# Neighbourhood attention on 64x64 quarters of the array, SSD norm scales spread by DMA, and another start, in a one-layer hybrid encoder

## The chip, the cores and the metric

The program runs on one core of one Trainium2 chip. The metric is the device time of one execution in microseconds; lower is better. All arithmetic results are float32; the large projections are written as three products of a rounded high part and a low remainder (fp32r operands), the small ones as plain float32 matmuls.

## The reference

One encoder layer for two sequences of 256 tokens, 1024 channels, handled together as 512 tokens. What matters here:

```python
x = x + 0.5 * swiglu(rms_norm(x, ffn1_norm), ffn1_w_gate, ffn1_w_up, ffn1_w_down)
u = rms_norm(x, mix_norm)
proj = u @ w_in
q_na, k_na, v_na, q_mem, z, xbc, dt_raw, gate_logits = split_sizes(proj, IN_SIZES)
...
o_na = neighborhood_attention(q_na, k_na, v_na, na_rpb)     # 16 heads of 64; grid of 4 rows x 64 columns
...
y_ssd = y_fwd + y_bwd + ssd_d[:, None] * xs                 # 32 heads of 64
y_ssd = y_ssd.reshape(bsz, t, D_INNER) * silu(z)
o_ssd = grouped_rms_norm(y_ssd, ssd_norm, SSD_GROUPS)       # 8 groups of 256 channels
...
merged = g_na*(o_na @ w_br_na) + g_ssd*(o_ssd @ w_br_ssd) + g_mem*(o_mem @ w_br_mem)
x = x + merged @ w_out
x = x + 0.5 * swiglu(rms_norm(x, ffn2_norm), ffn2_w_gate, ffn2_w_up, ffn2_w_down)

def neighborhood_attention(q, k, v, rpb):                   # for each row r, column block n of 16 queries
    s = einsum("bnqhd,brnkhd->bhnqrk", q_r, k_b) * scale     # keys: 4 rows x 32 columns = 128
    s = where(valid, s + bias, -1e30)                        # 16 columns of the 32 are valid for a query
    p = softmax(s over the 128 keys)
    o = einsum("bhnqrk,brnkhd->bnqhd", p, v_b)
```

## The kernel before

**Weights and the main matmuls.** Weights come from HBM in items of up to 512 KB (`fetch`, line 288) into a ring of nine buffers, eight items ahead. `ahead` rounds an item to a high part on ScalarE (line 320, tile `wh`) and leaves the remainder on VectorE (line 234, tile `wl`), at most three items ahead. TensorE then runs three 512-wide matmuls for each 128x128 block: high weights with the high part of the activations, high with low, low with high (lines 543 to 545, 565, 587 to 589, 607 to 609). The order of the work is the list `PLAN`. Work that is not in the list (norms, attention, SSD) is written as generators; after each entry of the list each of up to three (later four) active ones is advanced by one `yield`. A tile framework puts the instructions into each engine's queue in an order of its own, close to the written one, and each engine takes its queue in that order; so does SyncE, which issues all DMAs.

**The start** (`setup`, `warm`). SyncE loads the first eight channel tiles `x` and the first weights. `warm` (line 427) runs ten matmuls on a zeroed tile `af` meanwhile. `factor_x` multiplies a half of an `x` tile by the norm gain, rounded on ScalarE (line 249, tiles `sh`, `a2h`) and its remainder on VectorE (line 245, `sl`, `a2l`); `t_x` makes further combinations, and `t_squares` sums the squares of all `x` tiles (tile `sq`). The first two passes over the weights (`do_pl`, lines 607 to 609, tile `q`) take four chunks of 24 matmuls each. A small product, `sum` (line 504), which TensorE takes within the first chunk of the second pass, turns the sum of the squares into one value a token.

**Neighbourhood attention** (`t_na`, one generator for each of eight head pairs). The queries of two heads are transposed (line 952) and copied into two zeroed tiles `qbd`, block diagonal in the two heads, so that for each of four column blocks one 128x128 by 128x128 matmul gives the scores of both heads (line 984, tile `ns`). The bias tile is added on VectorE (line 245), a maximum is taken (989), ScalarE takes the exponentials, VectorE divides, TensorE transposes (1001, tile `nT`), ScalarE copies, and one 128x128 by 128x128 matmul a column block gives the outputs of both heads (1007, tile `no`), of which the diagonal quarters are kept. The two sequences (`b`) go one after the other, with three yields between. These small tiles and the transposed ones share a pool of three PSUM banks (`pd`).

**SSD norm** (end of `t_ssd`, eight groups). The squares are summed by `sum` (line 504), a reciprocal root is taken in small VectorE steps (`rsqrt`, lines 270 to 276), giving a value a token, spread over partitions. `spread` (line 512) makes four diagonal tiles `dg`, and `spread_mm` (line 521, tile `R`) multiplies them by a tile of ones, so that every partition holds the row of all 512 values. Two multiplications by `R` (line 245) follow. The groups below `KEEP` = 6 are then stored to HBM (`scr_o`).

Of the kernel before, what the change touches and what calls it, by code (L numbers as in the profile page):

```python
# [24 lines left out]
NEG = -1e30  # L25
KEY0 = (0, 8, 24, 32)
STRIP0 = (16, 8, 8, 0)
# [151 lines left out]
KEEP, EARLY, PG, LEND = 6, 4, 54, 4  # L179
# [3 lines left out]
class Layer:  # L183
# [126 lines left out]
    def ahead(self, ci):  # L310

        for i in range(self.n_split, min(ci + 3, len(ITEMS))):
            it = ITEMS[i]
            self.fetch(i + DEPTH)
# [5 lines left out]
            self.S.copy(hi[:, :n], t[:, :n])  # L320
# [54 lines left out]
    def setup(self):  # L375
# [18 lines left out]
        self.namask = c(8).rearrange("p (n k) -> p n k", n=4)  # L394
# [5 lines left out]
        self.scr_x = self.dr.tile([KD, 128, NT], F32, name="scr_x")  # L400
        self.scr_v = self.dr.tile([NT, D], F32, name="scr_v")
        self.scr_r = self.dr.tile([2, 32, 2, 256], F32, name="scr_r")
        self.scr_o = self.dr.tile([16, 128, NT], F32, name="scr_o")
        self.xs_start("ffn1")
        for k in range(KD):
            if k < 4:
                self.factor_x(1, k, k, 0)
                self.factor_x(0, k, k, 1)
            else:
                self.factor_x(2, k - 4, k, 0)  # L410
                self.factor_x(4, k - 4, k, 1)
            if k % 2 and k < 5:
                self.ahead(k // 2 - 2)
# [7 lines left out]
    def warm(self):  # L421

        z = self.g(p="af")
        self.G.memset(z, 0.0)
        ps = self.bank("wm")
        for _ in range(WARM):
            self.T.matmul(ps[:, :256], z[:, :128], z[:, :256], start=True, stop=True)
# [507 lines left out]
    def t_na(self, pr):  # L935
        V, S, T = self.V, self.S, self.T
        hf, lp = divmod(pr, 4)
        vt = [self.g(p="nv").rearrange("p (n c) -> p n c", n=4) for _ in range(2)]
        sv = self.scr_v
        for b in range(2):  # L940
            for n in range(4):
                src = bass.AP(sv.tensor, sv.offset + (b * 256 + KEY0[n]) * D + pr * 128, [[64 * D, 4], [D, 32], [1, 128]])
                self.nc.sync.dma_start(out=vt[b][:, n, :], in_=src)
        st = self.g(p="st")
        self.nc.sync.dma_start(out=st[:, :192], in_=self.a["strip"][pr])
        qbd = [self.g(p="qbd") for _ in range(2)]
        for z in qbd:
            self.G.memset(z, 0.0)
# [4 lines left out]
        pv = ps.rearrange("p (b r n c) -> p b n r c", b=2, r=4, n=4)  # L953
        for b in range(2):
            qv = qbd[b].rearrange("p (n h r c) -> p n h r c", n=4, h=2, r=4)
            for h in range(2):
                rows = slice(64 * h, 64 * h + 64)
                self.ts(qv[rows, :, h, :, :], pv[rows, b], self.par("qn", 0, rows), ALU.mult)
# [6 lines left out]
        bias = self.g(p="bi")  # L965
        bv = bias.rearrange("p (n r k) -> p n r k", n=4, r=4)
        sv4 = st[:, :192].rearrange("p (r k) -> p r k", r=4)
        for n in range(4):
            self.tt(bv[:, n], sv4[:, :, STRIP0[n]:STRIP0[n] + 32],
                    self.namask[:, n:n + 1, :].to_broadcast([128, 4, 32]), ALU.add)  # L970
        yield
        if pr < LEND:
            self.lent += 1
            on = self.pf.tile([128, 1024], F32R, tag="raw", name=self.name("on"))
            hi, lo = on[:, :512], on[:, 512:]
        else:
            hi, lo = self.g(F32R, "onh"), self.g(F32R, "onl")
        self.o[("on", pr)] = (hi, lo)
        for b in range(2):
            ps = self.bank("ns")  # L980
            q4 = qbd[b].rearrange("p (n q) -> p n q", n=4)
            kv = kT[:, b * 256:(b + 1) * 256].rearrange("p (r k) -> p r k", r=4)
            for n in range(4):
                T.matmul(ps[:, n * 128:(n + 1) * 128].rearrange("p (r k) -> p r k", r=4), q4[:, n, :],
                         kv[:, :, KEY0[n]:KEY0[n] + 32], start=True, stop=True)
            t_ = self.g(p="nt")
            self.stt(t_, ps, 0.125, bias, ALU.mult, ALU.add)
            mx, sm, rc = (self.small(4, "nm") for _ in range(3))
            V.tensor_reduce(out=mx, in_=t_.rearrange("p (n k) -> p n k", n=4), op=ALU.max, axis=AX.X, negate=True)
            for n in range(4):  # L990
                v = t_[:, n * 128:(n + 1) * 128]
                self.act(v, v, AF.Exp, bias=mx[:, n:n + 1], accum_out=sm[:, n:n + 1])
            yield
            V.reciprocal(rc, sm)
            for n in range(4):
                v = t_[:, n * 128:(n + 1) * 128]
                self.ts(v, v, rc[:, n:n + 1], ALU.mult)
            yield
            ps = self.bank("nT")
            for n in range(4):  # L1000
                T.transpose(ps[:, n * 128:(n + 1) * 128], t_[:, n * 128:(n + 1) * 128], self.ident)
            pT = self.g(p="npT")
            S.copy(pT, ps)
            yield
            ps = self.bank("no")
            for n in range(4):
                T.matmul(ps[:, n * 128:(n + 1) * 128], vt[b][:, n, :], pT[:, n * 128:(n + 1) * 128], start=True, stop=True)
            for h in range(2):
                rows = slice(64 * h, 64 * h + 64)
                ov = ps[rows].rearrange("p (n h q) -> p n h q", n=4, h=2)[:, :, h, :].rearrange("p n (r c) -> p n r c", r=4)  # L1010
                dst = lambda z: z[rows, b * 256:(b + 1) * 256].rearrange("p (r n c) -> p n r c", r=4, n=4)
                S.copy(dst(hi), ov)
                self.tt(dst(lo), ov, dst(hi).bitcast(F32), ALU.subtract)
            if b == 0:
                yield


    def do_gate(self, key, cis):
# [180 lines left out]
    def t_ssd(self, g):  # L1199
        V, S, T = self.V, self.S, self.T  # L1200
# [85 lines left out]
                y.append(q)  # L1286
            yield
        self.tt(y[0], y[0], y[1], ALU.add)
        ps = self.rows_to_cols(y[0])
        dg = self.spread(self.rsqrt(ps[:, 0:4], 4, 1.0 / 1024))  # L1290
        yield
# [28 lines left out]
def layout(inp):  # L1320
# [41 lines left out]
    qcol = n[None, :] * 16 + (i % 16)[:, None]  # L1362
    kcol = np.array(KEY0)[:, None] + kc[None]
    start = np.clip(qcol - 8, 0, 48)
    ok = (kcol[None] >= start[:, :, None]) & (kcol[None] < start[:, :, None] + 16)
    c[:, 1024:1152] = np.where(ok, 0.0, NEG).reshape(128, 128)

    rpb = f("na_rpb")[0]
    h = i // 64
    r = i // 16 % 4  # L1370
    rel = np.clip(np.arange(48)[None] - (i % 16)[:, None] - 1, 0, 30)
    row = np.arange(4)[None] - r[:, None] + 7
    strip = np.stack([rpb[(2 * pr + h)[:, None, None], row[:, :, None], rel[:, None, :]] for pr in range(8)])
    return {"w": w, "xT": chan("x_prompt", "x_sample"), "memT": chan("mem_prompt", "mem_sample"), "params": p,
            "consts": c, "strip": np.ascontiguousarray(strip.reshape(8, 128, 192))}


def build(arrays):
# [18 lines left out]
```

## Time and profile before

| | |
|---|---|
| median of 3 runs (lowest to highest) | 1771.69 us (1771.17 to 1771.84) |
| the profiled execution's own time | 1770.46 us |
| its span, from the first to the last instruction | 1768.7 us |
| TensorE matmuls busy | 1752.2 us, 99% of the span |
| VectorE, ScalarE, GpSimd busy | 71%, 48%, 1% |
| TensorE clock granted, mean | 0.998 |
| bytes moved by DMA | 206.77 MB, 117 GB/s on the mean |

Busy time of TensorE is a union of intervals whose ends are modelled, so it does not say that the array works at its peak. What a stage costs is read from the distance between the starts of its matmuls, and a float32 matmul (not fp32r) stands in the trace as two records, a transpose or an fp32r matmul as one. "L984" is line 984 of the kernel before. In a timeline a row gives start, length, engine, line and tiles (written tile, an arrow, read tiles), the count of merged records, and in brackets the idle time of the engine before it with what ended that.

### The profile page before, as it was taken

To read this page: it belongs to the slowest core of one execution; us is meant where nothing else is said; L and a number is where in the kernel's file an instruction comes from. 1 tells how busy PE (TensorE), PEld (TensorE's weight loads), DVE (VectorE), ACT (ScalarE), POOL (GpSimd) and SP (SyncE) were. 2 spreads that over 40 slices of the span, in tenths; PEclk is the share of its full clock that TensorE was granted. 3 is DMA by queue.
4 is the path that set the end of the run, shared out by engine and by line. 5 is a ranking of instruction groups with operands and counts; after the bars stand their busy time and mean duration, and the time that the engine had idled before them with its cause. 6 is when DMAs were issued, how large, how long until landed. Compare 5 with 4: busy or idle time off the path is not lost.

```text
span 1768.7 us, 22285 instructions
## 1 busy us (share of the span) xinstructions
PE 1752.2 (99%) x8348; PEld 1437.9 (81%) x8348; DVE 1252.4 (71%) x2128; ACT 855.3 (48%) x1530; POOL 9.0 (1%) x21
## 2 busy tenths in 40 slices
PE   8999999999999999999999999999999999999999
PEld 6888888988788888888787777777788878888887
DVE  7676776876554376857878988888743697776775
ACT  6444443543223335445656666667632464444442
POOL 0000000000000000000000000000000000000000
PEclk9999999999999999999999999999999999999999
DMA  6143334442323231323333433345434234244331
GB/s 254 48 150 131 101 110 141 155 155 80 96 84 100 80 115 58 105 88 98 119 119 124 138 131 120 113 143 173 143 127 136 84 98 140 84 144 130 98 117 48
DMA packets 75675, 206.77 MB, mean 117 GB/s; under 512 B 7856, under 2 KB 17456, under 8 KB 75568
## 3 DMA queue, kind: packets, MB, share of 16 engines
q1 hardware_dynamic: 75568, 205.36, 35.5%
q8 instruction: 65, 1.06, 0.2%
q14 instruction: 42, 0.34, 0.1%
HBM read 195.76 MB, written 9.57 MB: 116 GB/s over the span
## 4 chain that ended last, share of the span: by engine, by line
PE 96%; DVE 3%; DMA 1%; ACT 0%; issue 0%; SPq 0%; DVEq 0%; ACTq 0%
PE ac L565 20%; PE m L543 12%; PE m L545 12%; PE m L544 11%; PE q L587 5%; PE q L589 5%; PE q L588 5%; PE d L544 5%; PE d L545 5%; PE d L543 5%; PE y L1272 2%; PE hT L690 1%; DMA wr<-in_w 1%; DVE wl L234 1%; PE CB L1222 1%; PE q L608 1%
## 5 line engine op out<-in xcount | busy, mean ns | idle before, releaser
L320 ACT CAST wh<-wr 128x1024 fp32r<-128x1024 f32 (+1 forms) x357 | 371.3, 1040 | 689.2 <-PE ac L565 167.4
L234 DVE TENSOR_TENSOR wl<-wr,wh 128x1024 fp32r<-128x1024 f32 (+1 forms) x357 | 431.3, 1208 | 254.3 <-ACT wh L320 244.2
L543 PE MATMUL m<-uh,wh 128*128 128x512 f32 (+1 forms) x584 | 234.3, 401 | 1.4 <-ACT tg L249 1.4
L565 PE MATMUL ac<-wh,sh 128*128 128x512 f32 (+1 forms) x616 | 229.3, 373 | 0.8 <-ACT wh L320 0.8
L565 PE MATMUL ac<-wl,sh 128*128 128x512 f32 (+1 forms) x616 | 228.1, 370 | 0.7 <-DVE wl L234 0.7
L545 PE MATMUL m<-uh,wl 128*128 128x512 f32 (+1 forms) x584 | 228.4, 391 | 0.0
L544 PE MATMUL m<-ul,wh 128*128 128x512 f32 (+1 forms) x584 | 228.3, 391 | 0.0
L565 PE MATMUL ac<-wh,sl 128*128 128x512 f32 (+1 forms) x616 | 228.1, 370 | 0.0
L544 PE MATMUL d<-hl,wh 128*128 128x512 f32 x352 | 137.2, 390 | 0.7 <-DVE hl L234 0.7
L543 PE MATMUL d<-hh,wh 128*128 128x512 f32 x352 | 137.4, 390 | 0.5 <-ACT hh L256 0.5
L545 PE MATMUL d<-hh,wl 128*128 128x512 f32 x352 | 137.0, 389 | 0.0
L543 PEld LDWEIGHTS m<-uh,wh 128*128 128x128 f32 (+1 forms) x584 | 109.2, 187 | 30.7 <-issue 3.5
L565 PEld LDWEIGHTS ac<-wl,sh 128*128 128x128 f32 x616 | 116.1, 189 | 20.7 <-DVE wl L234 1.2
L565 PEld LDWEIGHTS ac<-wh,sh 128*128 128x128 f32 x616 | 116.0, 188 | 20.8 <-ACT wh L320 1.7
L565 PEld LDWEIGHTS ac<-wh,sl 128*128 128x128 f32 x616 | 116.1, 188 | 19.6
L545 PEld LDWEIGHTS m<-uh,wl 128*128 128x128 f32 (+1 forms) x584 | 109.2, 187 | 25.7 <-issue 1.5
L544 PEld LDWEIGHTS m<-ul,wh 128*128 128x128 f32 (+1 forms) x584 | 109.4, 187 | 21.9
L245 DVE SCALAR_TENSOR_TENSOR x<-d,x 128x512 f32<-128x512 f32 x96 | 66.2, 690 | 76.5 <-PE d L545 76.1
L234 DVE TENSOR_TENSOR wr<-wr,wr 128x1024 f32<-128x1024 f32 x80 | 97.6, 1220 | 6.6 <-DMA wr<-in_w 5.6
L587 PE MATMUL q<-wh,uh 128*128 128x512 f32 x256 | 101.9, 398 | 0.0
L589 PE MATMUL q<-wl,uh 128*128 128x512 f32 x256 | 99.9, 390 | 0.0
L588 PE MATMUL q<-wh,ul 128*128 128x512 f32 x256 | 99.8, 390 | 0.0
(252 smaller groups left out, 2932.1 us busy)
## 6 DMA issues: line engine op xcount, KB each, us to landing
wr<-in_w SPq DMA_DIRECT2D x308, 512.0 KB
rw<-scr_r SPq DMA_DIRECT2D x64, 256.0 KB
nv<-scr_v SPq DMA_DIRECT2D x64, 64.0 KB
scr_o<-cv SPq DMA_DIRECT2D x12, 256.0 KB
or<-scr_o SPq DMA_DIRECT2D x12, 256.0 KB
wr<-in_w SPq DMA_DIRECT2D x9, 256.0 KB
x<-in_xT SPq DMA_DIRECT2D x8, 256.0 KB
mr<-in_memT SPq DMA_DIRECT2D x8, 256.0 KB
```

The costliest lines, as they stand in the source:

```text
L234: self.V.tensor_tensor(out=out, in0=a, in1=b, op=op)
L245: self.V.scalar_tensor_tensor(out=out, in0=a, scalar=s, in1=b, op0=op0, op1=op1)
L320: self.S.copy(hi[:, :n], t[:, :n])
L543: self.T.matmul(ps[:m], wh[:, kk, :], xh, start=i == 0, stop=False)
L544: self.T.matmul(ps[:m], wh[:, kk, :], xl, start=False, stop=False)
L545: self.T.matmul(ps[:m], wl[:, kk, :], xh, start=False, stop=i == n - 1)
L565: go = lambda l, r, **f: self.T.matmul(ps, l, r, skip_group_check=True, **f)
L587: self.T.matmul(self.qb[t], xh, wh[:, kk, :], start=k == 0, stop=False)
L588: self.T.matmul(self.qb[t], xl, wh[:, kk, :], start=False, stop=False)
L589: self.T.matmul(self.qb[t], xh, wl[:, kk, :], start=False, stop=k == KD - 1)
L608: self.T.matmul(qb[t], xl, wh[:, kk, :], start=False, stop=False)
L1272: T.matmul(yb[64 * hp:64 * hp + 64, b * 256:(b + 1) * 256], xt[i][:, (2 * b + st) * 128 + 64 * hp:(2 * b + st) * 128 + 64 * hp + 64], w[hp ...
```

## The change

Four parts.

1. *Attention scores and outputs by quarters.* The queries of both heads stay on one tile (head h on partitions 64h to 64h+63). For each sequence, column block and head a matmul with 64 rows (one head's channels), 64 columns (64 queries) and 128 moving columns (keys) gives the scores; head h goes to its own PSUM bank, column blocks alternate between the lower and the upper 64 output partitions. The outputs take 64-column weights (one head's values of a block) and 64 moving columns, head h to output partitions 64h and up. Both sequences of a head pair go through in the same step, with three yields in all where there were seven. `qbd` is no longer zeroed. The bias comes laid out in full from the host.
2. *SSD norm, groups 0 to 5.* The 128x4 tile of scales is stored to HBM by one DMA (512 values of 4 bytes, token by token) and read back by a second one, spread over 128 partitions; the multiplication then reads that tile, two yields later. Groups 6 and 7 stay as they were.
3. *The start.* `factor_x` of a pair of `x` tiles stands right behind the loads of that pair, and `ahead` behind it; the weights beyond are fetched later (`self.depth`). A one-column ScalarE copy of the zeroed tile stands ahead of the idle matmuls and makes ScalarE load its function table then.
4. `WARM` goes from 10 to 16.

```diff
-RING, DEPTH, WARM = 9, 8, 10
+RING, DEPTH, WARM = 9, 8, 16
...
-        self.x = [self.g(p="x") for _ in range(KD)]
+        self.x, self.depth = [], 0
+        self.xs_start("ffn1")
         self.warm()
...
         for c in range(4):
             for k in (2 * c, 2 * c + 1):
+                self.x.append(self.g(p="x"))
                 dma(out=self.x[k], in_=self.a["xT"][:, k, :])
             self.fetch(c)
+            for k in (2 * c, 2 * c + 1):
+                for p, r in ((1, 0), (0, 1)) if c < 2 else ((2, 0), (4, 1)):
+                    self.factor_x(p, k % 4, k, r)
+            if c < 3:
+                self.ahead(c - 2)
+        self.depth = DEPTH
...
         z = self.g(p="af")
         self.G.memset(z, 0.0)
+        self.act(z[:, :1], z[:, 1:2], AF.Copy)
...
+        ps = [self.bank("ns") for _ in range(2)]
         for b in range(2):
-            ps = self.bank("ns")
...
             for n in range(4):
-                T.matmul(ps[:, n * 128:(n + 1) * 128].rearrange("p (r k) -> p r k", r=4), q4[:, n, :],
-                         kv[:, :, KEY0[n]:KEY0[n] + 32], start=True, stop=True)
+                g, c0 = n % 2, b * 256 + n // 2 * 128
+                for h in range(2):
+                    rows = slice(64 * h, 64 * h + 64)
+                    T.matmul(ps[h][64 * g:64 * g + 64, c0:c0 + 128].rearrange("p (r k) -> p r k", r=4),
+                             qT[rows, b * 256 + n * 64:b * 256 + n * 64 + 64], kv[rows, :, KEY0[n]:KEY0[n] + 32],
+                             start=True, stop=True)
...
-            for n in range(4):
-                T.matmul(ps[:, n * 128:(n + 1) * 128], vt[b][:, n, :], pT[:, n * 128:(n + 1) * 128], start=True, stop=True)
+        for b in range(2):
             for n in range(4):
+                c0 = b * 256 + n * 64
+                for h in range(2):
+                    T.matmul(ps[64 * h:64 * h + 64, c0:c0 + 64], vt[b][:, n, 64 * h:64 * h + 64], pT[h][:, c0:c0 + 64],
+                             start=True, stop=True)
...
-        dg = self.spread(self.rsqrt(ps[:, 0:4], 4, 1.0 / 1024))
-        yield
-        ps = self.spread_mm(dg)
+        r = self.rsqrt(self.rows_to_cols(y[0])[:, 0:4], 4, 1.0 / 1024)
+        if g < KEEP:
+            yield
+            self.link(99)
+            self.nc.sync.dma_start(out=self.scr_n[g].rearrange("t p -> p t"), in_=r)
+            ps = self.g(p="rw")
+            sn = self.scr_n
+            self.nc.sync.dma_start(out=ps, in_=bass.AP(sn.tensor, sn.offset + g * 512, [[0, 128], [1, 512]]))
+            yield
+            yield
+        else:
+            dg = self.spread(r)
+            yield
+            ps = self.spread_mm(dg)
```

What that makes of the engines' queues, at three places. First ScalarE at the very start, before (numbers are those of buffers; `x_83` to `x_90` are the eight `x` tiles in order, `wr` raw weights):

```order
L249 ACT_TABLE_LOAD
L249 ACTIVATE a2h_141<-x_83,params 128x256
L249 ACTIVATE a2h_141<-x_84,params 128x256
L320 CAST wh_153<-wr_107 128x1024
L249 ACTIVATE a2h_161<-x_85,params 128x256
L249 ACTIVATE a2h_161<-x_86,params 128x256
L249 ACTIVATE af_237<-x_83,params 128x512
L320 CAST wh_171<-wr_111 128x1024
L249 ACTIVATE sh_137<-x_83,params 128x256
```

and in the changed kernel (`x_105`, `x_107`, `x_127` are the first three `x` tiles):

```order
L249 ACT_TABLE_LOAD
L249 ACTIVATE af_84<-af_84 128x1
L249 ACTIVATE sh_111<-x_105,params 128x256
L249 ACTIVATE a2h_115<-x_105,params 128x256
L249 ACTIVATE sh_111<-x_107,params 128x256
L249 ACTIVATE a2h_115<-x_107,params 128x256
L320 CAST wh_123<-wr_109 128x1024
L249 ACTIVATE sh_133<-x_127,params 128x256
```

The tile `sh` of the first two `x` tiles, which the first main matmul reads, stood behind two casts of weights and a 512-wide multiplication; now it stands ahead of the first cast. The table load no longer has a wait ahead of it.

Second, TensorE at the scores of the first three head pairs, before:

```order
L984 MATMUL ns_5392<-kT_5322,qbd_5224 128x128 x4
L984 MATMUL ns_5408<-kT_5334,qbd_5249 128x128 x4
L984 MATMUL ns_5424<-kT_5346,qbd_5274 128x128 x4
```

and in the changed kernel (the last rows of the first pair, then the second and the third pair):

```order
L979 MATMUL ns_5376<-kT_5315,qbd_5237 64x128
L979 MATMUL ns_5377<-kT_5315,qbd_5237 64x128
L979 MATMUL ns_5413<-kT_5324,qbd_5257 64x128 x7
L979 MATMUL ns_5414<-kT_5324,qbd_5257 64x128 x7
L979 MATMUL ns_5413<-kT_5324,qbd_5257 64x128
L979 MATMUL ns_5414<-kT_5324,qbd_5257 64x128
L979 MATMUL ns_5450<-kT_5333,qbd_5277 64x128 x7
L979 MATMUL ns_5451<-kT_5333,qbd_5277 64x128 x7
```

Twelve matmuls on three banks became 48 on six, in one stretch; before, twelve more stood some hundred rows later for the other sequence. Where the two banks of a pair alternate, neighbours lie on different quarters of the array; in a run of seven on one bank they differ in the output half alone. Over the whole stage, the 128 score matmuls stand in six stretches and the 128 output matmuls in five.

Third, SyncE at an SSD group of the changed kernel; `scr_n` and the `rw` tile read from it are new, the other `rw` rows are rows that the SSD reads in any case:

```order
L288 DMA wr_8919<-in_w 128x1024
L288 DMA wr_8967<-in_w 128x1024
L1299 DMA scr_n<-y_8828 128x4x1
L1302 DMA rw_8897<-scr_n 128x512
L1202 DMA rw_8899<-scr_r 128x512
L1202 DMA rw_8951<-scr_r 128x512
L288 DMA wr_9033<-in_w 128x1024
```

Behind the store and the load back stand two row loads for the next group and the next weights; SyncE waits at the store for the scales and at the load for the store's landing.

More of the change, by code (lines that the diff above doesn't have):

```diff
@@ L313, in ahead @@
             it = ITEMS[i]
[L314 removed]
+            self.fetch(i + self.depth)
             self.sums(i + 1)
@@ L402, in setup @@
         self.scr_r = self.dr.tile([2, 32, 2, 256], F32, name="scr_r")
+        self.scr_n = self.dr.tile([8, 4, 128], F32, name="scr_n")
         self.scr_o = self.dr.tile([16, 128, NT], F32, name="scr_o")
[L404 to L413, printed above, removed]
         for k in range(4):
@@ L943, in t_na @@
                 self.nc.sync.dma_start(out=vt[b][:, n, :], in_=src)
[L944 to L948, printed above, removed]
+        bias = self.g(p="bi")
+        self.nc.sync.dma_start(out=bias, in_=self.a["strip"][pr])
         cs = slice(lp * 128, (lp + 1) * 128)
@@ L953, in t_na @@
         pv = ps.rearrange("p (b r n c) -> p b n r c", b=2, r=4, n=4)
+        qT = self.g(p="qbd")
         for b in range(2):
[L955 to L958, printed above, removed]
+            self.ts(qT[:, b * 256:(b + 1) * 256].rearrange("p (n r c) -> p n r c", n=4, r=4), pv[:, b], self.par("qn"), ALU.mult)
         yield
@@ new lines, in t_na @@
+                for h in range(2):
[3 more added lines that the diff above has]
+                             start=True, stop=True)
+        t_ = [self.g(p="nt") for _ in range(2)]
+        sm = [self.small(4, "nm") for _ in range(2)]
+        for h in range(2):
+            two = lambda z: z.rearrange("p (b k) -> p b k", b=2)
+            self.stt(two(t_[h]), two(ps[h]), 0.125,
+                     bias[:, h * 256:(h + 1) * 256].unsqueeze(1).to_broadcast([128, 2, 256]), ALU.mult, ALU.add)
+            mx = self.small(4, "nm")
+            V.tensor_reduce(out=mx, in_=t_[h].rearrange("p (n k) -> p n k", n=4), op=ALU.max, axis=AX.X, negate=True)
+            for n in range(4):
+                v = t_[h][:, n * 128:(n + 1) * 128]
+                self.act(v, v, AF.Exp, bias=mx[:, n:n + 1], accum_out=sm[h][:, n:n + 1])
@@ L995, in t_na @@
+        yield
+        for h in range(2):
+            rc = self.small(4, "nm")
+            V.reciprocal(rc, sm[h])
             for n in range(4):
-                v = t_[:, n * 128:(n + 1) * 128]
+                v = t_[h][:, n * 128:(n + 1) * 128]
                 self.ts(v, v, rc[:, n:n + 1], ALU.mult)
-            yield
-            ps = self.bank("nT")
+        yield
+        pT = []
+        for h in range(2):
+            p = self.bank("nT")
             for n in range(4):
-                T.transpose(ps[:, n * 128:(n + 1) * 128], t_[:, n * 128:(n + 1) * 128], self.ident)
@@ L1002, in t_na @@
[L1002 to L1005, printed above, removed]
-            for n in range(4):
[L1007 to L1013, printed above, removed]
@@ L1014, in t_na @@
-            if b == 0:
-                yield
+                T.transpose(p[:, n * 128:(n + 1) * 128], t_[h][:, n * 128:(n + 1) * 128], self.ident)
+            t = self.g(p="npT")
+            S.copy(t, p)
+            pT.append(t)
+        yield
+        ps = self.bank("no")
+        for b in range(2):
+            for n in range(4):
+                c0 = b * 256 + n * 64
+                for h in range(2):
+                    T.matmul(ps[64 * h:64 * h + 64, c0:c0 + 64], vt[b][:, n, 64 * h:64 * h + 64], pT[h][:, c0:c0 + 64],
+                             start=True, stop=True)
@@ L1018, in do_gate @@
+        for b in range(2):
+            ov = ps[:, b * 256:(b + 1) * 256].rearrange("p (n r c) -> p n r c", n=4, r=4)
+            dst = lambda z: z[:, b * 256:(b + 1) * 256].rearrange("p (r n c) -> p n r c", r=4, n=4)
+            S.copy(dst(hi), ov)
+            self.tt(dst(lo), ov, dst(hi).bitcast(F32), ALU.subtract)
     def do_gate(self, key, cis):
@@ L1362, in layout @@
     qcol = n[None, :] * 16 + (i % 16)[:, None]
+    start = np.clip(qcol - 8, 0, 48)
     kcol = np.array(KEY0)[:, None] + kc[None]
-    start = np.clip(qcol - 8, 0, 48)
     ok = (kcol[None] >= start[:, :, None]) & (kcol[None] < start[:, :, None] + 16)
-    c[:, 1024:1152] = np.where(ok, 0.0, NEG).reshape(128, 128)
+    gh = np.arange(2)[:, None] + 2 * np.arange(2)[None]
+    mask = np.where(ok, 0.0, NEG).reshape(2, 64, 4, 32)
+    c[:, 1024:1088] = np.concatenate([mask[g][:, gh[g]] for g in range(2)]).reshape(128, 64)
     rpb = f("na_rpb")[0]
-    h = i // 64
     r = i // 16 % 4
-    rel = np.clip(np.arange(48)[None] - (i % 16)[:, None] - 1, 0, 30)
+    col = np.array(STRIP0)[gh][:, :, None] + kc - np.zeros((1, 1, 1), int)
+    rel = np.clip(col[i // 64] - (i % 16)[:, None, None] - 1, 0, 30)
     row = np.arange(4)[None] - r[:, None] + 7
-    strip = np.stack([rpb[(2 * pr + h)[:, None, None], row[:, :, None], rel[:, None, :]] for pr in range(8)])
+    strip = np.stack([rpb[hd][row[:, None, :, None], rel[:, :, None, :]].reshape(128, 256) for hd in range(16)])
+    strip = strip.reshape(8, 2, 128, 256).transpose(0, 2, 1, 3)
     return {"w": w, "xT": chan("x_prompt", "x_sample"), "memT": chan("mem_prompt", "mem_sample"), "params": p,
-            "consts": c, "strip": np.ascontiguousarray(strip.reshape(8, 128, 192))}
+            "consts": c, "strip": np.ascontiguousarray(strip.reshape(8, 128, 512))}
 def build(arrays):
```

22 lines of the change are left out of this document (6 added, 16 removed).

## The prediction

> **What bounds the kernel now.** I read the page first: the span, the engines' busy shares and the chain that ended last.
>
> ```profile
> span 1768.7 us, 22285 instructions
> PE 1752.2 (99%) x8348; PEld 1437.9 (81%) x8348; DVE 1252.4 (71%) x2128; ACT 855.3 (48%) x1530; POOL 9.0 (1%) x21
> ...
> PE 96%; DVE 3%; DMA 1%; ACT 0%; issue 0%; SPq 0%; DVEq 0%; ACTq 0%
> ```
>
> TensorE carries 96% of the chain. So a change counts by the matmul time that it takes away, and by the stalls of TensorE that it ends or makes. Where those are is told by TensorE's own waits (what waited, for what; us in total, times, longest):
>
> ```profile
> PE q L607 <- ACT sh L249: 4.8, 1, 4.8
> PE m L543 <- ACT tg L249: 1.4, 1, 1.4
> PE wm L427 <- POOL af L424: 1.3, 1, 1.3
> PE q L608 <- DVE sl L245: 1.1, 1, 1.1
> ```
>
> All other entries are 0.8 us or less. Outside the first 20 us there is next to nothing to win by waiting less; in attention and SSD only fewer or faster matmuls pay. The start is read from a view by stretches (length, PE busy and records, granted clock, DMA share, GB/s) and the timeline:
>
> ```profile
> 7.72:12.50 4.78, 0.00 (x0) 0.93 1.02 396
> 12.50:18.40 5.90, 4.76 (x10) 0.50 1.04 408
> 18.40:21.80 3.40, 3.40 (x16) 0.96 1.04 414
> ```
>
> ```profile
> 0.73 0.52 POOL L424 MEMSET af<- 128x512 f32 x1 [0.29 <-POOLq L1381]
> 1.31 6.41 PE L427 MATMUL wm<-af 128*128 128x256 f32 x20 [1.31 <-POOL af L424]
> 4.20 1.28 ACT L249 ACT_TABLE_LOAD   x1 [4.20 <-DMA x<-in_xT]
> 8.37 1.04 ACT L320 CAST wh<-wr 128x1024 fp32r<-128x1024 f32 x1 [1.97 <-DMA wr<-in_w]
> 9.45 1.23 DVE L234 TENSOR_TENSOR wl<-wr,wh 128x1024 fp32r<-128x1024 f32 x1 [2.53 <-ACT wh L320]
> 12.51 0.80 PE L607 MATMUL q<-wh,sh 128*128 128x512 f32 x1 [4.80 <-ACT sh L249]
> 14.44 0.79 PE L608 MATMUL q<-wh,sl 128*128 128x512 f32 x1 [1.13 <-DVE sl L245]
> 21.77 0.39 PE L607 MATMUL q<-wh,sh 128*128 128x512 f32 x1
> 21.99 0.39 PE L608 MATMUL q<-wh,sl 128*128 128x512 f32 x1
> ```
>
> The idle matmuls end at 7.7; the array is idle until 12.51 and then runs at half clock to 18.4. The first weights are there at 8.37, cast at 9.41, their remainder done at 10.68. What comes later is the order: `sh` and `sl` of the first tiles stand behind other work. The second chunk of 24 matmuls starts at 21.77; from there matmuls start 0.227 us apart.
>
> **The start: worked out.** In the changed kernel ScalarE's table load (1.28 us) has no wait, so it ends about 2.0 when it starts like the other engines at 0.73. The idle matmuls wait for the small copy behind it, so they start about 2.3 instead of 1.31. Sixteen of them are 32 records; the stretch from 1.31 to 5.00 holds nine records (0.41 us each, as at half clock), the rest of the twenty 0.22 us each. With the clock rising at the same 5.0: six slow records, 26 fast ones of 0.217, end at 10.7. `sh`, `sl` of two tiles are ready before the cast at 8.37, `wl` at 10.7. So the first chunk runs from 10.7 at full clock: 24 x 0.227 = 5.4, second chunk at 16.1 instead of 21.77, 5.6 us sooner. No engine gets less work, and the next thing late is VectorE:
>
> ```profile
> 36.72 3.08 DVE L234 TENSOR_TENSOR sq<-sq,sq 128x512 f32<-128x512 f32 x4 [0.39 <-ACT sq L249]
> 39.85 1.05 PE L504 MATMUL sum<-consts,sq 128*128 128x1 f32 x8 [0.24 <-DVE sq L234]
> ```
>
> VectorE is busy nearly without a break from 9.45 to the last of the four square sums, 39.7. TensorE must wait there, since `sum` stands in its queue. In the new order the queue takes 15 matmuls of the second pass before `sum`, not 6. TensorE would be at `sum` at 16.1 + 3 x 5.45 + 15 x 0.227 = 35.9. VectorE does two remainders (0.8 us) earlier than before and loses fewer gaps, so I put its last sum at 37.5: `sum` comes 2.3 us earlier and nine matmuls (2.0 us) lie ahead of it already. **Gain 4.3 us**; at best 5.6 (no wait at `sum`), at least 2.0 (VectorE as late as before, the nine matmuls alone). Should the clock fall none the less, 24 matmuls at half speed cost 5.4 us and the gain is near nothing.
>
> **Attention: worked out.** The scores and outputs of three head pairs, and the same lines grouped by form:
>
> ```profile
> 660.27 2.84 PE L984 MATMUL ns<-kT,qbd 128*128 128x128 f32 x24
> 662.87 0.48 PE L587 MATMUL q<-wh,uh 128*128 128x512 f32 x1
> ...
> 680.67 2.84 PE L1007 MATMUL no<-npT,nv 128*128 128x128 f32 x24
> 683.27 0.48 PE L587 MATMUL q<-wh,uh 128*128 128x512 f32 x1
> ```
>
> ```profile
> L984 PE MATMUL ns<-kT,qbd 128*128 128x128 f32 x128 | 16.2, 275 | 0.0
> L1007 PE MATMUL no<-npT,nv 128*128 128x128 f32 x128 | 16.0, 275 | 0.0
> L1272 PE MATMUL y<-e,xt 128*64 128x256 f32 x256 | 39.6, 393 | 0.0
> L847 PE MATMUL am<-qkT,qkT 128*128 128x256 f32 x64 | 14.5, 379 | 0.0
> ```
>
> 24 records take 2.60 us, 108 ns each; the 256 of both lines take 27.7 us. After the change there are 256 matmuls, 512 records. Whether neighbours on different parts of the array run together decides. The trace has one such case, `y`: two 64-column halves in turn, 256 moving columns. A record of it costs 39.6/256 = 155 ns of busy time, one on the whole array (`am`) 14.5/64 = 227. In place:
>
> ```profile
> 868.45 0.39 PE L545 MATMUL m<-uh,wl 128*128 128x512 f32 x1
> 868.77 1.08 PE L1272 MATMUL y<-e,xt 128*64 128x256 f32 x8
> 869.78 0.50 PE L543 MATMUL m<-uh,wh 128*128 128x512 f32 x1
> ```
>
> Eight records in 1.01 us where eight in turn would take 1.8: two run together. The rest, 0.10 behind and 0.09 ahead (868.77 against 868.45 + 0.227), is the price of a stretch in another tiling, 0.19.
>
> Scores: 256 records of 128 moving columns. One after another 27.7; two together 13.8; four together 6.9. In the new order 84 of the 128 matmuls alternate over four quarters, 44 over two: 168/4 x 0.108 + 88/2 x 0.108 = 9.3. Outputs: 256 records of 64 moving columns on two halves. The nearest row for so short a record is a transpose:
>
> ```profile
> 498.69 0.22 PE L1133 MATMUL dtT<-consts,dt 64*128 64x64 f32 x1
> 498.76 0.22 PE L1134 MATMUL dtT<-consts,dt 64*128 64x64 f32 x1
> ```
>
> 0.062 us apart. Two together: 128 x 0.062 = 7.9; at best half of 108, 6.9; one after another 15.9. Stretches: 11 x 0.19 = 2.1. Banks: three must serve six tiles in the first stretch, so TensorE waits there for VectorE to empty one (0.64 each, `nt`, below) and at the transposes for ScalarE; the crowded places are the first stretch, its transposes, and two later pairs. I take 3.5 in all; bounds 0 and 16 banks x 0.64 = 10.
>
> ```profile
> 664.80 1.28 DVE L245 SCALAR_TENSOR_TENSOR nt<-ns,bi 128x512 f32<-128x512 f32 x2
> 666.00 0.67 DVE L989 TENSOR_REDUCE nm<-nt 128x4 f32<-128x512 f32 x1
> ```
>
> Sum 9.3 + 7.9 + 2.1 + 3.5 = 22.8 against 27.7: **gain 4.9 us**. Bounds: 6.9 + 6.9 + 2.1 = 15.9 (gain 11.8), and with everything in turn 27.7 + 15.9 + 2.1 + 3.5 = 49.2 (loss 21.5). Fewer and fuller VectorE and ScalarE instructions, and no zeroing on GpSimd, lie beside TensorE and count nothing; the exponentials of both sequences now come at once (24 instead of 12 in a round) and have 48 main matmuls, 10.9 us, as cover.
>
> **SSD norm: worked out.**
>
> ```profile
> L521 PE MATMUL R<-dg,consts 128*128 128x128 f32 x72 | 10.9, 283 | 0.0
> ...
> L512 DVE TENSOR_SCALAR dg<-consts,y x36: 270/281/290, 382.4 to 1280.6; 128x128 f32<-128x128 f32 x36
> ...
> SPq L1384 <- DMA out<-x: 1.7, 1, 1.7
> ```
>
> Of nine users of `R`, six groups go: 48 records x 108 ns = 5.2 us of TensorE. In its place, per group, a store and a load. The final store of the kernel is waited for 1.7 us after its issue of 0.3, so a pair is 4 us when nothing is in its way; a store of 512 pieces may take more, and weights stand ahead in the queue. The multiplication that needs the row stands in VectorE's queue behind nine instructions (a remainder `wl` of 1.2, others of 0.3 to 0.7), 5 to 6 us. When the load is late, VectorE waits, and behind it stand the convolution and the decay products that `y` needs; TensorE has split weights for two more units (2 x 24 x 0.227 = 10.9 us). SyncE holds two row loads and a weight load back for those 4 us; weights are eight items ahead. I take 0.2 us: **gain 5.0 us**; bounds 5.4 (the two tilings that `R` parts) and nothing (0.9 us lost a group).
>
> The Trainium skill, page "DMA: Bandwidth & Descriptors", section "Rules for kernel authors", says that a strided last dimension becomes one descriptor for each element; by it the store is 512 descriptors of 4 bytes, and the load is late rather than early. No run here shows such a store yet.
>
> **Sum.** 4.3 + 4.9 + 5.0 = 14.2. The profiled execution took 1770.46 us, 1.2 below the median; from the median 1771.7 that is **1757.5 us**.
>
> **Rivals.**
>
> *Two together, never four, and a start that VectorE holds.* `y` shows two halves; no row shows two row halves side by side. Scores then cost 13.8 (4.5 more) and the start gains 3: 1757.5 + 4.5 + 1.3 = 1763.3. Against it: nothing in the rows tells row halves from column halves.
>
> *A record every 62 ns, whatever its size.* The transposes of 64 columns start 0.062 apart though half of 108 would do; if that is the rate at which matmuls are handed out, 512 records take 31.7 us, 4.0 more than before, with stretches 2.1 and, as the banks then have time to empty, 1 of waits: loss 7.1 instead of gain 4.9, time 1769.5. For it is the even 0.062; against it that the weights of 128 columns may set that pace, and that `y` puts two records into one slot.
>
> The Trainium skill, page "TensorE: Matmul & The Clock Gate", section "Wait — 56ns, not 53.3ns?", gives about 62 ns a matmul for the sequencer when hardware decode is off, as the bound for short matmuls; the trace's 0.062 agrees in number, and no row here has enough short records in a row to tell it from a load of weights.
>
> *Quarters in turn (slower than before).* If the quarters do not overlap, because both head halves read the same moving path and their weights load one by one, attention costs 49.2: 21.5 - 4.3 - 5.0 = 12.2 us slower, 1784. It decides once a record takes over (27.7 + 9.3 - 5.6)/512 = 61 ns on the mean. `y` speaks against it for the output halves, nothing for the row halves.
>
> *The norm does not do what it says.* VectorE waits 1 us and more a group for the load and TensorE feels it: 5 us back, 1762.5.
>
> **How the numbers follow.** Forecast 0.46; two together 0.25; 62 ns 0.13; in turn 0.06; norm lost 0.10. The forecast's own range is 1752 to 1763. The wide one starts at 1750.5, a little short of attention and the start both at their best (1757.5 - 6.9 - 1.3 = 1749.3), and ends at 1768, short of the last part of the 62 ns case. Faster by over 0.2% (below 1768.2; about what a measurement of this kernel tells from no change): forecast, two together, norm lost, and a third of the 62 ns case, 0.85; within 0.2%: the rest of that case, 0.08; slower: 0.07.
>
> **What would show it.** The start: granted clock 1.0 throughout, second chunk at about 16, `sum` at about 37.5 with a wait on `sq` ahead of it. Attention: records of the first head pair's scores bunched in fours, 0.9 us for its 32; 62 ns even steps speak for that rival, 108 for turns. Waits of TensorE for `nt` at the second and third pair. SSD: 24 records of `R` left, and no TensorE wait in that stage. I am wrong if TensorE's distance between starts outside these three places changes, or if the clock falls at the start.

## The result: slower by 0.6%, and the profile after

The changed kernel takes 1780.88 us in the median of four runs (1779.25 to 1783.05), the kernel before 1771.43 beside it (1769.11 to 1771.84). The ratio is 1.0057, with a 95% interval of 1.0039 to 1.0074. I had forecast 1757.5 and a range of 1750.5 to 1768. The profiled execution took 1783.05 us.

Head and chain of the page of the changed kernel, then TensorE's waits (what waited, for what; us in total, times, longest):

```profile
span 1781.2 us, 22578 instructions
PE 1750.0 (98%) x8568; PEld 1426.1 (80%) x8568; DVE 1230.8 (69%) x2056; ACT 848.0 (48%) x1515; POOL 0.7 (0%) x5
...
PE 84%; DVE 7%; DMA 5%; issue 1%; ACT 1%; SPq 0%; DVEq 0%; ACTq 0%
```

```profile
PE y L1278 <- DVE e L234: 7.6, 5, 5.2
PE xT L1217 <- DVE cv L245: 7.0, 4, 2.2
PE ns L979 <- DVE nt L245: 3.3, 1, 3.3
PE wm L427 <- ACT af L249: 2.3, 1, 2.3
```

The chain ran through TensorE for 96% of the span; now it is 84%, with VectorE and DMA in between. TensorE is busy 2.2 us less, but there are two new waits in SSD (`y` and `xT`, 14.6 us) and one in attention.

**The start** goes nearly as forecast (timeline of the changed kernel, and one stretch of it with TensorE's busy time and records, clock, DMA share, GB/s):

```profile
2.28 8.97 PE L427 MATMUL wm<-af 128*128 128x256 f32 x32 [2.28 <-ACT af L249]
10.90 0.58 PE L607 MATMUL q<-wh,sh 128*128 128x512 f32 x1
16.57 0.39 PE L607 MATMUL q<-wh,sh 128*128 128x512 f32 x1
37.54 1.05 PE L504 MATMUL sum<-consts,sq 128*128 128x1 f32 x8 [1.08 <-DVE sq L234]
```

```profile
10.90:16.60 5.70, 5.70 (x27) 1.00 1.05 408
```

First chunk at 10.90 at full clock, second at 16.57 instead of 21.77, `sum` at 37.54 after a wait for the squares. From 43 us on the same main matmul starts 4.4 us sooner than before.

**Attention.** One head pair's scores in a row, and then the first stretch, where three pairs come at once:

```profile
701.80 1.10 PE L979 MATMUL ns<-kT,qbd 64*64 64x128 f32 x32
702.83 0.50 PE L543 MATMUL m<-omh,wh 128*128 128x512 f32 x1
```

```profile
656.04 1.96 PE L979 MATMUL ns<-kT,qbd 64*64 64x128 f32 x46
661.25 4.72 PE L979 MATMUL ns<-kT,qbd 64*64 64x128 f32 x50 [3.25 <-DVE nt L245]
665.90 0.79 PE L587 MATMUL q<-wh,uh 128*128 128x512 f32 x1
```

```profile
661.20:668.00 6.80, 6.75 (x55) 5.76 (x56) 5.64 (x10) 5.08 (x26) 0.00 (x0) 0.51 0.02 7
```

Alone, 32 records take 1.03 us: four quarters do run together. In the first stretch 96 records take 9.86 us where three times 1.03 would do. TensorE stands 3.25 us until VectorE has emptied a bank, the clock granted afterwards is 0.51 (the last fence is that stretch in the view by stretches; the clock stands before the DMA share), and the records of the second and third pair mostly run two together, since their order alternates over two quarters only.

**SSD.** Four views of the changed kernel: SyncE's timeline at a group, VectorE's there, VectorE's waits, and the chain at another group (start, length, what):

```profile
930.80 0.39 SPq L1299 DMA_DIRECT2D scr_n<-y  x1
939.65 0.34 SPq L1302 DMA_DIRECT2D rw<-scr_n  x1
940.04 0.90 SPq L1202 DMA_DIRECT2D rw<-scr_r  x2
```

```profile
943.56 1.42 DVE L245 SCALAR_TENSOR_TENSOR cv<-cv,half,rw 128x512 f32<-128x512 f32 x2 [4.45 <-DMA rw<-scr_n]
```

```profile
DVE cv L245 <- DMA rw<-scr_n: 34.2, 6, 6.8
```

```profile
985.14 8.42 DMA scr_n<-y
993.56 0.02 issue
993.58 0.33 SPq L1302
993.91 0.05 issue
993.96 6.71 DMA rw<-scr_r
1000.67 0.02 issue
1000.69 0.51 ACT e L249
1001.20 0.53 ACT ct L249
1001.73 0.02 issue
1001.75 0.70 DVE cv L245
1002.45 0.14 issue
1002.59 1.05 PE xT L1217 x4
```

The store of 2 KB in 512 pieces takes 8.4 us at the group in the chain. At the other one the load back is issued 8.85 us after the store (930.80 to 939.65); SyncE stands at it nearly all that time, with two row loads behind it that have nothing to do with the norm. VectorE stands at the multiplication (4.45 us here, 34.2 in six groups). At the group in the chain it is not even the norm's own row that ends last: it is a row load held behind it, then ScalarE's exponential, then the convolution, then TensorE.

### The profile page after: what moved, and what is told of

Its sections match the earlier page's. It is cut to its first block, busy times and chain, and to the rows that moved or that the text cites. A ratio compares the mean times of both kernels' runs of the same rounds, so it can differ in the third digit from the quotient of the medians.

```text
span 1781.2 us, 22578 instructions
## 1 busy us (share of the span) xinstructions
PE 1750.0 (98%) x8568; PEld 1426.1 (80%) x8568; DVE 1230.8 (69%) x2056; ACT 848.0 (48%) x1515; POOL 0.7 (0%) x5
## 2 busy tenths in 40 slices
DMA packets 79708, 209.69 MB, mean 118 GB/s; under 512 B 11120, under 2 KB 19696, under 8 KB 79600
## 4 chain that ended last, share of the span: by engine, by line
PE 84%; DVE 7%; DMA 5%; issue 1%; ACT 1%; SPq 0%; DVEq 0%; ACTq 0%
PE ac L565 21%; PE m L543 9%; PE m L545 9%; PE m L544 9%; PE q L587 5%; PE q L589 5%; PE q L588 5%; PE d L544 4%; PE d L545 4%; PE d L543 4%; DMA scr_n<-y 3%; DVE cv L245 2%; DVE wl L234 2%; DMA rw<-scr_r 2%; PE y L1278 1%; DVE e L245 1%
## 5 line engine op out<-in xcount | busy, mean ns | idle before, releaser
L249 ACT ACTIVATE e<-rw,lots 128x256 f32<-128x256 f32 (+1 forms) x256 | 97.8, 444 | 46.3 <-DMA rw<-scr_r 46.3
```

The costliest lines, as they stand in the source:

```text
L249: self.S.activation(out=out, in_=x, func=f, **kw)
```

## The experiments

All times are medians on the same chips as the kernel before (1770.1 to 1770.4 in these three sets).

### One part at a time

*The start alone.* The kernel before with `setup`, `warm`, `ahead` and `WARM` of the change.

```diff
-RING, DEPTH, WARM = 9, 8, 10
+RING, DEPTH, WARM = 9, 8, 16
...
+        self.x, self.depth = [], 0
+        self.xs_start("ffn1")
...
```

> The kernel before with parts 3 and 4 (the start) alone. Theory: the first pass runs 4.5 us sooner, as the distance between the same matmuls in the two traces shows from 43 us on, and nothing takes it back: 1771.4 - 4.5 = 1767. Rival: the earlier start is lost again at a later wait, since VectorE has the same work: 1771. PE's granted clock at 5 to 20 us is 1.0 under both.

1766.91 us, ratio 0.9979 (0.9970 to 0.9988): 3.5 us faster. In the profiled execution the same main matmul is 4.1 us sooner from 43 us to 1270. At 1292 TensorE then waits 1.42 us for ScalarE (`osh`), which it did not before, and the lead is 2.8 us at the end. So the gain holds for the most part; in that execution the rival has a third of it.

*Start and attention*, the change without the norm's part.

```diff
-        if g < KEEP:
-            yield
...
-        else:
-            dg = self.spread(r)
-            yield
-            ps = self.spread_mm(dg)
+        dg = self.spread(self.rsqrt(ps[:, 0:4], 4, 1.0 / 1024))
+        yield
+        ps = self.spread_mm(dg)
```

> The change without part 2: groups 0 to 5 of the SSD norm go through the diagonal tiles as before. Theory: the whole loss sits in the norm's trip through HBM; start 4.5 and attention 3 are left: 1764, with a TensorE wait for the biased scores of 3.3 us in attention's first stretch. Rival A: the attention part loses what it wins, because of that wait and the half clock behind it: 1767. Rival B: part of the 20 us that SSD lost comes from the order that start and attention hand on to it: 1770 or more.

1765.79 us, ratio 0.9975 (0.9966 to 0.9984). The norm's loss is gone, so it does not come from what start and attention hand on. But attention has won 1.1 us between the medians, less than the two intervals can tell from nothing: rival A.

*The norm alone*, on the kernel before.

```diff
+        if g < KEEP:
...
+            self.nc.sync.dma_start(out=self.scr_n[g].rearrange("t p -> p t"), in_=r)
...
+            self.nc.sync.dma_start(out=ps, in_=bass.AP(sn.tensor, sn.offset + g * 512, [[0, 128], [1, 512]]))
...
```

> The kernel before with part 2 (the norm's scales through HBM) alone. Theory: the norm alone loses about 20 us, 1771 + 20 = 1791, VectorE waits about 34 us for the loaded rows in six places and TensorE some 15 us for VectorE. Rival: the norm alone is harmless or a gain, as predicted (1766), and only the new attention or start made it late: 1766 to 1776.

1800.05 us, ratio 1.0167 (1.0153 to 1.0181): 29.7 us slower, half as much again as the theory said. Here already the first group costs TensorE 8.7 us in one piece:

```profile
940.94 1.94 PE L1273 MATMUL y<-e,xt 128*64 128x256 f32 x6 [8.68 <-DVE e L234]
938.98 1.49 ACT L249 ACTIVATE e<-rw,lots 128x256 f32<-128x256 f32 x4 [7.57 <-DMA rw<-scr_r]
```

ScalarE had no rows for the next heads, since their loads stood behind the store. In the changed kernel ScalarE waits 6.2 us for rows at the same group too, but TensorE's wait for `y` there stays under 1 us. The order tells the two apart: with the norm alone, TensorE has about 30 main matmuls between the first store's issue and the `y` that waits; in the changed kernel the store comes about 50 main matmuls later, and about 80 lie between it and the `y` that waits. The 8.68 us, and 5.2 us at half clock behind them (a granted clock of 0.50 from 940.94 to 946.10), make some 11 of the 16 us by which the norm's part costs more here (30 us) than in the changed kernel (14).

### The form of the store

*Sixteen bytes a piece.* The changed kernel with `scr_n` as 128x4 a group: one line of the store, one of the multiplication. The order on every engine stays.

```diff
-            self.nc.sync.dma_start(out=self.scr_n[g].rearrange("t p -> p t"), in_=r)
+            self.nc.sync.dma_start(out=self.scr_n[g], in_=r)
...
-            self.stt(v, v, self.half[:, 2 * g + i:2 * g + i + 1], ps, ALU.mult, ALU.mult)
+            pv, vv = (ps.rearrange("p (q t) -> p t q", t=4), v.rearrange("p (t q) -> p t q", t=4)) if g < KEEP else (ps, v)
+            self.stt(vv, vv, self.half[:, 2 * g + i:2 * g + i + 1], pv, ALU.mult, ALU.mult)
```

> The changed kernel with one difference: the store of the 128x4 tile writes 16 bytes a partition in one piece (partition-major), the load back is as before, and VectorE's multiplication reads the row with a stride of four. All engines keep their order. Theory 1, the 512 pieces of 4 bytes are what takes long: the time between store issue and load issue falls from 8.9 to about 3 us, VectorE's waits for the row from 34 to under 5 us, time 1764 - 5 = 1759. Theory 2, SyncE's wait for any store's landing is what it is: 8.9 and 34 us stay, 1781. Theory 3, half and half: a short store still holds the row loads behind it for some 4 us: VectorE waits 10 to 15 us, time 1766.

1760.78 us, ratio 0.9947 (0.9935 to 0.9960): theory 1. SyncE at the same group:

```profile
930.96 0.33 SPq L1299 DMA_DIRECT2D scr_n<-y  x1
934.57 0.33 SPq L1302 DMA_DIRECT2D rw<-scr_n  x1
```

3.6 us instead of 8.85, VectorE no longer waits for the row loaded from `scr_n`, and TensorE's waits at `y` and `xT` are gone. Against the kernel without the norm's part (1765.8) it is 5.0 us faster.

*Eight bytes a piece*, 256 pieces; VectorE multiplies in two halves.

```diff
+            self.nc.sync.dma_start(out=self.scr_n[g].rearrange("a p b -> p a b"), in_=r.rearrange("p (a b) -> p a b", a=2))
...
```

> The kernel with the 16-byte store, but the store writes 256 pieces of 8 bytes (two tokens' groups of a partition side by side), and VectorE multiplies in two halves. Theory, the store's time goes by the number of pieces: store issue to load issue was 8.9 us with 512 and 3.6 with 128 pieces, so 3.6 + 5.3/3 = 5.4 us with 256; VectorE's wait about 2 us a group and the time 1764 to 1768. Rival, only a piece below some size is slow, or the whole is a step: 3.6 or 8.9 us.

1763.27 us, ratio 0.9970 (0.9955 to 0.9986); its five runs lie from 1760.66 to 1768.02, so its distance from the 16-byte store (1760.78) is not clear of the noise. From store issue to load issue, mean of the six groups:

| pieces | bytes each | store issue to load issue, us |
|---|---|---|
| 128 | 16 | 3.1 (2.7 to 3.6) |
| 256 | 8 | 4.4 (3.6 to 5.0) |
| 512 | 4 | 9.1 (8.4 to 9.6) |

The time grows with the pieces, but not in a straight line (5.1 was due at 256 by these means): 10 ns for each further piece at first, 18 after. VectorE waits 6.5 us in six places, about half of what the expectation had. Whether number or size of the pieces does it, these three cannot tell, since both change. The trace's records of single packets narrow it down: with 128, 256 and 512 pieces alike, the last piece's record starts 2.1 to 2.6 us after the store's issue. So the difference lies behind these records, between the last piece and the landing; what takes the time there the trace does not show.

### Which of the two waits costs the time

*The load one yield later* and *the multiplication three yields later*, both with the slow store.

```diff
             self.nc.sync.dma_start(out=self.scr_n[g].rearrange("t p -> p t"), in_=r)
+            yield
             ps = self.g(p="rw")
...
-            yield
             yield
```

> The changed kernel (store in 4-byte pieces) with the load back issued one yield after the store, so that SyncE can issue the row loads and weights of that yield before it waits for the store; the multiplication stays where it was. Theory SyncE (what ends last is a row load held behind the waiting load): TensorE's waits in SSD mostly vanish, about 1767. Theory VectorE (what ends last is VectorE standing at the multiplication, with the convolution and decay products behind it): the row comes no sooner, VectorE waits 30 us or more in six places, 1776 to 1782.

```diff
             yield
             yield
+            yield
+            yield
+            yield
```

> The changed kernel (store in 4-byte pieces, load right behind it) with the multiplication three yields later (five instead of two). Theory VectorE: its wait for the row vanishes and with it TensorE's, 1760 to 1764. Theory SyncE: the row loads of the next heads still stand some 9 us behind the store's landing; the exponentials and y are late, TensorE keeps half or more of its waits in SSD, 1770 or more.

1782.01 (ratio 1.0066, 1.0052 to 1.0079) and 1778.79 (1.0052, 1.0039 to 1.0065): neither helps. The first is no test of SyncE's queue: the framework put the load right behind the store again and one row load ahead of both, so SyncE stood as long as before (932.17 to 941.21). The second did what it was meant to: VectorE no longer waits for the norm's row, but for ScalarE, and ScalarE for row loads (VectorE's waits, then ScalarE's timeline):

```profile
DVE cv L245 <- ACT ct L249: 36.1, 5, 8.1
```

```profile
946.89 0.51 ACT L249 ACTIVATE e<-rw,lots 128x256 f32<-128x256 f32 x1 [8.90 <-DMA rw<-scr_r]
```

One wait has taken the place of the other, almost of the same sum (34.2 before).

*Store and load from GpSimd's queue*, with the slow store, and the same *with the multiplication three yields later*.

```diff
-            self.nc.sync.dma_start(out=self.scr_n[g]...
+            self.nc.gpsimd.dma_start(out=self.scr_n[g]...
-            self.nc.sync.dma_start(out=ps, in_=bass.AP(sn.tensor, ...
+            self.nc.gpsimd.dma_start(out=ps, in_=bass.AP(sn.tensor, ...
```

> The changed kernel (4-byte pieces) with the store of the scales and the load back issued by GpSimd, which has nothing else to do there; SyncE then holds back no row load and no weight. VectorE multiplies at the same place as in the changed kernel. If what costs is SyncE's queue alone: TensorE's waits in SSD vanish, 1762 to 1766. If VectorE's standing at the multiplication is enough by itself: it waits 4 us or more in six places as before, 1774 to 1782.

> As the run before, on GpSimd's queue, and VectorE multiplies three yields later. The delay alone left the time at 1779, since the row loads stood behind the store (VectorE then waited 36 us for ScalarE, and ScalarE for rows). Theory, both waits are links of their own and each alone is enough for the loss: with both removed TensorE's waits in SSD vanish though the store is as slow as before, 1760 to 1765. Rival: the 512 pieces of 4 bytes slow other transfers or the store takes longer from GpSimd's queue than the delay covers: 1770 or more.

1788.90 us (ratio 1.0107, 1.0091 to 1.0123) and 1760.31 us (0.9947, 0.9933 to 0.9961). In the first the loss stays and grows. TensorE waits for VectorE, and VectorE for the row:

```profile
PE xT L1217 <- DVE cv L245: 20.7, 6, 4.9
```

```profile
DVE cv L245 <- DMA rw<-scr_n: 48.2, 6, 9.9
SPq L1313 <- DVE cv L245: 64.8, 11, 12.6
```

SyncE no longer stands at the store's landing, but it is not free: it stands 64.8 us at the stores to `scr_o`, which need VectorE's product (second row). ScalarE waits for row loads only once, 7.8 us, so what TensorE loses comes by VectorE. With both cured the loss is gone, although the store is no faster at all:

```profile
931.17 0.89 POOL L1299 DMA_DIRECT2D scr_n<-y  x1 [929.91 <-DVE e L245]
942.72 0.55 POOL L1302 DMA_DIRECT2D rw<-scr_n  x1 [10.66 <-DMA scr_n<-y]
```

```profile
949.61 0.74 DVE L245 SCALAR_TENSOR_TENSOR cv<-cv,half,rw 128x512 f32<-128x512 f32 x1
```

The row is multiplied 18 us after the store's issue, and VectorE has not stopped for it. So the store's slowness is not the loss in itself. It becomes one by two ways, SyncE's queue (the multiplication later, 1778.79) and VectorE's (GpSimd's queue, 1788.90), and each is enough alone.

### Attention: three banks for six tiles

*A stagger* of 0, 1, 2 yields ahead of the scores by head pair, and *twice as much* (0, 2, 4; `range(2 * (pr % 3))`), both on the kernel with the 16-byte store.

```diff
+        for _ in range(pr % 3):
+            yield
         ps = [self.bank("ns") for _ in range(2)]
```

> The kernel of the run before (store in 16-byte pieces, 1760.8) with one or two extra yields ahead of the scores, by the head pair's number modulo 3, so that the first three pairs no longer ask for six PSUM banks at once. Theory: attention's gain is eaten by three banks serving six tiles. In the run without the norm's part the stage costs 24.5 us for scores and outputs, of which the first stretch of 96 records takes 9.9 where 3 x 1.03 = 3.1 would do, and transposes, half clock and others another 3; with the stretch broken up 5 to 8 us come back: 1753 to 1756. Rival: the banks are as short wherever the stretches lie (transposes and outputs want them too), and the waits only move: 1759 to 1761.

> As the run with the stagger, with twice the yields (0, 2, 4), so that nearly every stretch of scores has 16 matmuls of one pair. Theory of banks: at least as fast as the single stagger, 1752 to 1756, and the score records cost 32 ns each throughout (eight pairs x 1.03 us = 8.3 us in all). Rival: the longer way of each pair pushes work towards the end of the stage, where TensorE must wait for the last pair: 1757 or more.

1760.79 us (ratio 0.9948, 0.9935 to 0.9960) and 1754.25 us (0.9910, 0.9896 to 0.9923). The small stagger only moves the wait, as the rival had it:

```profile
669.93 1.04 PE L1007 MATMUL nT<-consts,nt 128*128 128x128 f32 x8
670.89 0.65 PE L981 MATMUL ns<-kT,qbd 64*64 64x128 f32 x6
674.48 1.97 PE L981 MATMUL ns<-kT,qbd 64*64 64x128 f32 x26 [2.94 <-ACT npT L1009]
```

The third pair's scores now stand right behind the transposes of the first, and wait until ScalarE has copied those out of their bank. With twice the distance no wait for a bank is left, and 6.5 us come back. The sums below are TensorE's times from each record's start to the next one's, in us, between the same two of the main matmuls (1200 of them, from the first `qT` on):

| | start alone | start and attention | 16-byte store, double stagger |
|---|---|---|---|
| scores | 13.9 | 16.3 | 10.6 |
| outputs | 14.0 | 8.2 | 8.7 |
| transposes `nT` | 6.2 | 7.6 | 7.5 |
| transposes `qT`, `kT` | 5.0 | 5.4 | 5.6 |
| 1200 main matmuls | 280.2 | 281.2 | 280.4 |
| others | 17.8 | 18.7 | 18.5 |
| sum | 337.1 | 337.4 | 331.3 |

The outputs gave nearly all that was forecast. The scores lost more in the first stretch than they won elsewhere, the transposes `nT` took 1.4 more, and the main matmuls, some of them at half clock, 1.0 more.

### All eight groups by DMA

```diff
-        if g < KEEP:
+        if True:
...
```

> The fastest kernel so far (16-byte store, stagger 0, 2, 4; 1754.3) with groups 6 and 7 of the norm through HBM as well. Theory: 24 records of the product with ones go, 24 x 0.108 = 2.6 us, of which some 0.5 come back as store and load behind the last group have less cover: 1752 to 1753. Rival: behind the last group the multiplication is wanted at once, TensorE waits for the trip of some 7 us: 1756 to 1760.

1757.14 us, ratio 0.9924 (0.9911 to 0.9937), on the kernel of 1754.25. No gain is to be seen. The time lies where the rival had it, with VectorE waiting 6.7 us for the row at two groups and TensorE 2.6 us for ScalarE (`osh`) and 1.5 us at `y`; but the two intervals overlap, so whether it is slower stays open.

The best is the kernel with 16-byte store and double stagger: 1754.25 us, 15.9 less than the kernel before beside it.

## Why the prediction was wrong

The three parts, in medians of the runs, each kernel against the kernel before beside it (before to start alone, to start and attention, to the change):

| part | forecast gain, us | measured gain, us |
|---|---|---|
| start | 4.3 | 3.5 (4.1 to 5.1 between the profiles) |
| attention | 4.9 | 1.1, or none |
| SSD norm | 5.0 | -14.0 |

**The start: right**, step by step. The idle matmuls waited for the table load to 2.28 (2.3), the first chunk stood at 10.9 (10.7), the second at 16.57 (16.1), `sum` at 37.54 (37.5), the clock at 1.0.

**Attention: the mechanism right, one term too small.** The terms for scores, outputs and stretches, 9.3 + 7.9 + 2.1 = 19.3, are what the double stagger shows (10.6 and 8.7 with the stretches' edges, 19.3 in all). Every rival on the array itself fell. Records of neighbouring quarters start 7 ns apart and a group of four every 109 ns; the outputs start in pairs every 59 ns. So the mean distance is 27 and 30 ns. The 62 ns a matmul that the Trainium skill's page "TensorE: Matmul & The Clock Gate", section "Wait — 56ns, not 53.3ns?", has for a sequencer without hardware decode is not what binds here: a matmul of two records takes 54 ns in the scores and 59 in the outputs, the latter only little less. The step that failed is "I take 3.5 in all; bounds 0 and 16 banks x 0.64 = 10" for the banks. By the table (start and attention against the start alone) it came to about 8.9, near the upper bound: scores and outputs took 24.5 instead of 19.3, the transposes 1.8 more, main matmuls and others 1.9 more. I had counted the time in which VectorE empties a bank as if it came at once. In fact VectorE was behind: it had a 1.22 us `wl` and a late bias tile (3.78 us of waiting for it) ahead of the first `nt`. With the start alone it reaches the first `nt` no sooner (660.62 against 660.51 here), but there the next scores stand much later and no bank is missed. And I had not counted that TensorE runs at half clock behind its 3.25 us stall.

```profile
658.10 0.76 DVE L234 TENSOR_TENSOR bi<-bi,consts 128x256 f32<-128x256 f32 x2 [3.78 <-DMA bi<-in_strip]
...
659.38 1.22 DVE L234 TENSOR_TENSOR wl<-wr,wh 128x1024 fp32r<-128x1024 f32 x1
660.51 1.28 DVE L245 SCALAR_TENSOR_TENSOR nt<-ns,bi 128x512 f32<-128x512 f32 x2
```

**The norm: wrong, and it decides.** The gain on TensorE is real: with the 16-byte store it is 5.0 us. That it meets the forecast to the tenth is luck: in the two traces the 48 records of `R` took 7.0 us from start to start, not 48 x 0.108 = 5.2, and the main matmuls took 1.8 more without them. The step that failed is the price of the trip: "a pair is 4 us when nothing is in its way; a store of 512 pieces may take more", and then "I take 0.2 us ... bounds 5.4 and nothing". The trip took 12.8 us (930.80 to 943.56), of which 8.85 passed before the load back could be issued. The rule that I had quoted, of the Trainium skill's page "DMA: Bandwidth & Descriptors", section "Rules for kernel authors" (one descriptor for each element), spoke against the change, and the trace agrees with it: the page of the changed kernel counts 79708 packets, that of the kernel with the 16-byte store 77404, which is 2304 or 6 x (512 - 128) fewer. The same bytes in a quarter of the pieces landed in about a third of the time. But I had let it change nothing in the sum. I took the row of an undisturbed store of another form for the price, though it was the nearest only in kind. Worse was the lower bound. I had named both places where it could bite, VectorE's queue and the row loads behind SyncE, and yet closed the range at a lost gain, as if a wait could cost no more than the work that it replaces. A wait in the queue of an engine that feeds TensorE showed no such bound here: VectorE's 34.2 us and the row loads made 14.6 us of TensorE's waits. Behind one of them, of 1.94 us at 1002.59, the clock was 0.51 for 3.4 us, and behind the last, 5.16 us long, it was 0.50 for 6 us, which makes some 4.7 us more:

```profile
1225.30:1231.30 6.00, 5.99 (x16) 4.03 (x17) 6.00 (x12) 5.18 (x13) 0.00 (x0) 0.50 1.03 394
```

The rival "the norm does not do what it says" had the right place and side, and 5 us where about 19 were lost (the 5.0 of the gain and 14.0 beyond).

## What to carry to other kernels

A short transfer is priced by its form, and by who stands behind it: before moving work from the engine that sets the end to a trip through HBM, write down the landing time of that very form, then every instruction behind the wait on the queue that issues it and on the engine that reads it, and shorten the trip or cure both. When tiles are packed more densely onto the array, count the PSUM banks that one stretch of the queue asks for; if they don't suffice, spread the users in time until the one before has been emptied. A gain on the engine that sets the end can be real and still be paid back nearly fourfold by a stall that was not there before.

## What the hardware showed beside that

- 64x64 quarters of the array run four at a time in float32: 32 records of 128 moving columns in 1.03 us, where the 128x128 form took 2.60 us for 24.
- A store of 2 KB took 3.1, 4.4 and 9.1 us to the issue of the load that waits for it with 128, 256 and 512 pieces, though the last piece's record starts 2.1 to 2.6 us after the issue in all three. Issued by GpSimd, the 4-byte store took 10.6 us (mean of the six groups of both kernels), and there it stands in the trace as 16 packets of 128 bytes.
- In the changed kernel stalls of 3.25 us in attention and 1.94 and 5.16 us in SSD were followed by 3.4 to 6 us at half clock; one of 2.21 us (at 1115.90) was followed by none.
